# A Mamba-2 layer on one core: the first output block regrouped with fillers and a drain, x's sum forms at other steps, and a dt chain with priority and other banks

## The chip, the core and the metric

The kernel runs on one core of a Trainium2 chip. The metric is the device time of one execution in microseconds (us), the median over runs. The engines in the text are PE (matrix products), DVE (vector operations), ACT (activations), POOL and SP. SP only issues transfers here.

## The reference

One layer of a Mamba-2 mixer over a sequence of L = 512 tokens, all in float32:

```
h = rmsnorm(x)                        # x: 512 x 2048
z, x', B, C, dt = split(h @ w_in)     # 4096, 4096, 8*128, 8*128, 64 columns
x', B, C = silu(conv4(x', B, C))      # causal, 4 taps
dt = softplus(dt + bias)
a = dt * -exp(a_log)                  # decay of each of 64 heads
y = chunked scan: y_diag = (C B^T * exp(cs_l - cs_s)) (x' dt),  y_off = exp(cs) C state
y = rmsnorm((y + D x') * silu(z)) @ w_out
out = rmsnorm(x + y)
```

cs is the running sum of a in a chunk.

## The kernel before, in words

**Numbers.** Each float32 operand is a pair of rounded parts: hi (made by ACT, L88) and lo = value - hi (made by DVE, L89). A product is three matmuls: hi by hi, hi by lo, lo by hi. A weight arrives as a raw piece of 512 KB (buffers ra, rb, rc; three, one and two of them), and `split_piece` splits it. PE can start on a piece when hi is there, and goes on to the third matmul when lo is.

**Order.** PE, SP and POOL follow the order in which the program is written. ACT and DVE are ordered by a scheduler from dependences and priorities; `urgent` raises the priority. The written order is a table of steps: `add(step, function)` puts an event at a step, `run(step)` issues all events of that step between two pieces of PE work. A step is six matmuls, about 0.7 us when PE does not wait.

**The first stage: eight plain tiles** of 128 projection columns each (B, C, x, z, x, z, B, C), two pieces a tile, eight steps a piece. The tiles 2 to 7 begin at step 32, so step 80 begins the second piece of tile 4 and step 120 the second piece of tile 7. Beside them run:

- `x_forms(g, j)`: a quarter of three combinations of x's quadrants (forms 1, 2 and 4), from raw x loaded again: two loads, four ACT scalings, then on DVE L576, L577, L579 and three L574. At steps 49, 56, 63 and 70. `x_form3(j)` makes the fourth form in place over x's right half (L588 to L592), with the conv's buffer xr as scratch, at steps 114, 118, 122 and 126.
- The dt chain: `dt_softplus` at step 58 (L346 to L364), `dt_cumul` at 91 (cs, L372), `dt_sums` at 94 (nwl, win), `dt_spread` at 96 (transposes of cs, copy into sn at L389, store to DRAM as cscr, exponentials, store as escr). These use the one bank of `ps_tr` (tag tr), which xd's transposes (L486) use too.
- Then the first unit's scan: `u_load` brings cscr back, spread over 128 rows, as csb; `u_decay` makes the decay matrix m from it (L469 to L472 on ACT, L474 on DVE). `g_cb` multiplies C by B (cbm, L449).

**The quads** come from step 128 on: pairs of tiles by 2x2 Strassen products (seven instead of eight) over the combined x; T1, T2, T3, R11, R21 and so on name a product. Their weights are sums of pieces (L618).

**The output** (L139): `blocks` is a list of pieces (s, pairs), one accumulation group a tuple, or a pair of tiles by Strassen (`opair`). Of the block's plain groups each of four row tiles t is added into acc (L1065). Between two Strassen pairs the last product of one runs inside the next as filler (`prev`). The combinations of y for the pair are fetched and made by `y_fetch` and `y_forms` (f1, f11 and so on, L860). `load_y(p)` brings y back from DRAM (yscr) and splits it: y2 becomes ybh and ybl.

Of the kernel before, what the change touches and what calls it, by code (L numbers as in the profile page):

```python
# [35 lines left out]
def mamba_layer(ctx: ExitStack, tc: tile.TileContext, d: dict, out: bass.AP):  # L36
# [102 lines left out]
    blocks = [[(0, (0,))] + every(0, 1)[1:] + [(0, (1, 2))] + every(2)[1:], (2, 3), every(3, 12), (4, 5),  # L139
# [234 lines left out]
    def dt_sums():  # L374
        pl = ps_tr.tile([P, NC, H], F32, name="tr")
# [7 lines left out]
    def dt_spread():  # L383
        pct = ps_tr.tile([H, NC, P], F32, name="tr")
# [170 lines left out]
    def x_forms(g, j):  # L555
# [8 lines left out]
        if j == 0:  # L564
# [17 lines left out]

    def x_form3(j):

        kk = slice(2 * j, 2 * j + 2)
        h, lo = xh[:, kk, hi_], xl[:, kk, hi_]
        t = xr[:, 3:L + 3].rearrange("p (k l) -> p k l", k=2)
        V.tensor_tensor(out=t, in0=xh[:, kk, lo_], in1=h, op=ALU.subtract)  # L588
        V.tensor_tensor(out=t, in0=t, in1=xl[:, kk, lo_], op=ALU.add)
        V.tensor_tensor(out=t, in0=t, in1=lo, op=ALU.subtract)  # L590
        S.copy(out=h, in_=t)
        V.tensor_tensor(out=lo, in0=t, in1=h, op=ALU.subtract)  # L592
# [137 lines left out]
    steps = {0: [66, 71, 63, 104, 104, 114], 1: [56, 76, 72, 108, 108, 114], NU - 1: [36, 46, 44, 65, 65, 71]}  # L730
# [298 lines left out]
    for kb, blk in enumerate(blocks[:-1]):  # L1029
# [10 lines left out]
        for s, pairs in blk:  # L1040
            ps = [None] * NC
            for p in pairs:
# [4 lines left out]
                for t in range(NC):  # L1047
# [106 lines left out]
```

## Time and profile before

| | us |
|---|---|
| median of 3 runs (1267.62 to 1270.22) | 1269.15 |
| the profiled execution | 1271.58 |
| its span in the trace | 1269.6 |
| PE busy | 1235.1 (97%) |
| DVE busy | 1079.0 (85%) |
| ACT busy | 829.0 (65%) |
| POOL busy | 77.6 (6%) |

The span is what the trace covers; the 2.0 more of its execution lie around it. A row of the trace gives the start, the duration, the engine, the line, the operation and the tiles (out<-in). In brackets stands the engine's idle time before it and what ended that. PE's clock as granted is 1.00 at full speed; durations of PE are longer where it is lower.

### The profile page before, as it was taken

How to read it: one execution, taken by the hardware profiler on the slowest of the kernel's cores; microseconds unless marked ns; L12 is line 12 of the kernel's file. 1: busy time of each engine (PE TensorE's matmuls, PEld its weight loads, DVE VectorE, ACT ScalarE, POOL GpSimd, SP SyncE). 2: the span in 40 equal slices, each digit the busy share in tenths (PEclk: the TensorE clock that was granted, in tenths of full speed). 3: DMA queues.
4: the chain of work that ended last, by engine and by line, in shares of the span. 5: the costliest groups of instructions: out<-in, count | busy, mean ns of one | idle time of the engine just before them, and what ended most of it. 6: DMA issues, size and time to landing. Idle time of an engine off the chain costs nothing.

```text
span 1269.6 us, 24517 instructions
## 1 busy us (share of the span) xinstructions
PE 1235.1 (97%) x9945; PEld 1178.0 (93%) x9945; DVE 1079.0 (85%) x1443; ACT 829.0 (65%) x1359; POOL 77.6 (6%) x99
## 2 busy tenths in 40 slices
PE   8989899999999999999999999999999899999997
PEld 7989899999999999999999999999888899899986
DVE  5796989998999998899989899988857887887865
ACT  7666677767767767876686777678666445444533
POOL 0000000010000000000001000000000000000000
PEclk9989999999999999999999999999999999999998
DMA  9546656767676667667676766775537576657612
GB/s 357 181 150 180 169 157 174 189 173 193 166 194 182 156 193 189 169 162 197 178 203 151 210 163 176 184 184 153 157 114 253 155 197 202 208 127 229 183 60 100
DMA packets 70193, 225.89 MB, mean 178 GB/s; under 512 B 8384, under 2 KB 12800, under 8 KB 69952
## 3 DMA queue, kind: packets, MB, share of 16 engines
q1 hardware_dynamic: 56688, 176.34, 39.5%
q0 software_dynamic: 12672, 46.14, 23.0%
q8 instruction: 78, 1.28, 0.4%
q10 hardware_dynamic: 720, 1.84, 0.4%
q14 instruction: 35, 0.29, 0.1%
HBM read 211.52 MB, written 12.78 MB: 177 GB/s over the span
## 4 chain that ended last, share of the span: by engine, by line
PE 61%; DVE 19%; ACT 8%; DMA 6%; issue 5%; SPq 0%; DVEq 0%; ACTq 0%
PE S L649 5%; PE S L651 5%; PE S L650 5%; DVE lo L89 4%; PE R L649 4%; PE R L650 3%; PE R L651 3%; PE mm L651 3%; PE mm L649 3%; PE mm L650 3%; PE mm L948 3%; PE mm L950 3%; PE mm L949 3%; PE mm L886 3%; PE mm L887 2%
## 5 line engine op out<-in xcount | busy, mean ns | idle before, releaser
L89 DVE TENSOR_TENSOR lo<-ra,hi 128x1024 fp32r<-128x1024 f32 x150 | 182.8, 1219 | 48.2 <-ACT hi L88 48.0
L88 ACT CAST hi<-ra 128x1024 fp32r<-128x1024 f32 x150 | 156.7, 1046 | 89.9 <-PE mm L887 23.5
L88 ACT CAST hi<-rc 128x1024 fp32r<-128x1024 f32 x94 | 98.9, 1053 | 99.0 <-PE mm L650 37.9
L649 PE MATMUL R<-s,hi 128*128 128x256 f32 x576 | 162.5, 282 | 0.0
L651 PE MATMUL mm<-xh,lo 128*128 128x256 f32 x576 | 159.2, 276 | 0.2 <-DVE lo L89 0.2
L649 PE MATMUL mm<-xh,hi 128*128 128x256 f32 x576 | 159.2, 276 | 0.2 <-ACT mm L705 0.2
L650 PE MATMUL R<-s,hi 128*128 128x256 f32 x576 | 159.2, 276 | 0.0
L651 PE MATMUL R<-s,lo 128*128 128x256 f32 x576 | 159.1, 276 | 0.0
L650 PE MATMUL mm<-xl,hi 128*128 128x256 f32 x576 | 159.1, 276 | 0.0
L89 DVE TENSOR_TENSOR lo<-rc,hi 128x1024 fp32r<-128x1024 f32 x94 | 114.3, 1216 | 3.9 <-ACT hi L88 3.7
L649 PEld LDWEIGHTS mm<-xh,hi 128*128 128x128 f32 x576 | 108.2, 188 | 0.6 <-ACT mm L705 0.6
L651 PEld LDWEIGHTS mm<-xh,lo 128*128 128x128 f32 x576 | 108.1, 188 | 0.4 <-DVE lo L89 0.4
L650 PEld LDWEIGHTS R<-s,hi 128*128 128x128 f32 x576 | 108.3, 188 | 0.0
L649 PEld LDWEIGHTS R<-s,hi 128*128 128x128 f32 x576 | 108.3, 188 | 0.0
L651 PEld LDWEIGHTS R<-s,lo 128*128 128x128 f32 x576 | 108.1, 188 | 0.0
L650 PEld LDWEIGHTS mm<-xl,hi 128*128 128x128 f32 x576 | 108.1, 188 | 0.0
L618 DVE TENSOR_TENSOR ra<-ra,rc 128x1024 f32<-128x1024 f32 x88 | 107.0, 1216 | 0.2
L651 PE MATMUL S<-xh,lo 128*128 128x256 f32 x288 | 79.7, 277 | 2.2 <-DVE lo L89 2.2
L649 PE MATMUL S<-xh,h1h 128*128 128x256 f32 x288 | 80.3, 279 | 1.0 <-ACT mm L705 1.0
L650 PE MATMUL S<-xl,hi 128*128 128x256 f32 x288 | 79.7, 277 | 0.7 <-DVE xl L592 0.7
L650 PE MATMUL S<-xl,h1h 128*128 128x256 f32 x288 | 80.3, 279 | 0.0
L651 PE MATMUL S<-xh,h1l 128*128 128x256 f32 x288 | 80.3, 279 | 0.0
(452 smaller groups left out, 3936.0 us busy)
## 6 DMA issues: line engine op xcount, KB each, us to landing
rc<-in_wi SPq DMA_DIRECT2D x76, 512.0 KB, 5.2
ra<-in_wi SPq DMA_DIRECT2D x42, 512.0 KB, 6.0
rb<-in_wi SPq DMA_DIRECT2D x40, 512.0 KB, 4.6
ra<-in_wi POOLq DMA_DIRECT2D x36, 512.0 KB, 6.2
rb<-in_wi POOLq DMA_DIRECT2D x36, 512.0 KB, 6.2
csb<-cscr SPq DMA_DIRECT2D x32, 512.0 KB, 5.6
ra<-in_wo SPq DMA_DIRECT2D x26, 512.0 KB, 5.2
yscr<-z SPq DMA_DIRECT2D x32, 256.0 KB, 4.4
```

Source lines behind the costliest of these rows:

```text
L88: S.copy(out=hi, in_=raw)
L89: V.tensor_tensor(out=lo, in0=raw, in1=hi, op=ALU.subtract)
L618: V.tensor_tensor(out=raw, in0=raw, in1=qs[n][other], op=ALU.add)
L649: T.matmul(ps, hi[:, k, :], ah, start=first and k == 0, stop=False, skip_group_check=True)
L650: T.matmul(ps, hi[:, k, :], al, start=False, stop=False, skip_group_check=True)
L651: T.matmul(ps, lo[:, k, :], ah, start=False, stop=k == KH - 1, skip_group_check=True)
L886: T.matmul(ps[:, t, :], yh[:, k, tt], hi[:, k, :], start=st, stop=False, skip_group_check=True)
L887: T.matmul(ps[:, t, :], yl[:, k, tt], hi[:, k, :], start=False, stop=False, skip_group_check=True)
L948: T.matmul(ps, yh, hi, start=first and k == 0, stop=False)
L949: T.matmul(ps, yh, lo, start=False, stop=False)
L950: T.matmul(ps, yl, hi, start=False, stop=last and k == 1)
```

## The change

It has three parts.

1. **Output.** The first block's pieces are grouped anew: seven accumulation groups instead of eight, in the order s = 0, 1, 2, 3, 1, 2, 0. The last two tiles of the block's last piece are left out of the block and run inside the first Strassen pair, which so gets a filler (`bridge`) and the product order 11, 1, filler, 2, 4, 12, 3 instead of 1, 11, 4, 2, 12, 3. Its y forms move with the block, as does `load_y(2)`. After the block `T.drain()` stands in place of a spare transpose.
2. **x's forms.** `x_forms` runs at steps 38, 45, 66 and 92 in the order of quarters (1,1), (0,1), (0,0), (1,0). `x_form3` reads raw x, loaded once more by `x_diff` (512 KB at steps 106, 109, 122 and 124, into a buffer ra) and subtracted in place, and needs no scratch. It stands at steps 115, 118, 136 and 140.
3. **dt.** The four parts of the chain run with raised priority. The sums use the bank of `ps_yd`, the spread that of `ps_yo`. `g_cb` for group 0 moves from step 69 to 73, `u_decay` of unit 1 from 140 to 156.

On DVE, where the split of the second piece of tile 4 (lo<-rb) and the copy of cs stand. Before, from the end of dt_softplus on (the split of lo<-rb stands seven rows ahead of this):

```order
L359 SCALAR_TENSOR_TENSOR bt<-bt 128x256
L656 TENSOR_TENSOR z<-S,rbc 128x512
L361 SCALAR_TENSOR_TENSOR dt<-bt,z 128x256
L579 SCALAR_TENSOR_TENSOR rc<-rc,h1l 128x512
L364 SCALAR_TENSOR_TENSOR bt<-dt,dab 128x256
L574 TENSOR_TENSOR s_834<-rc,s_833 128x512
L89 TENSOR_TENSOR lo<-rc,hi 128x1024
L411 TENSOR_TENSOR xr<-mm,rbc 128x512
L574 TENSOR_TENSOR s_836<-rc,s_835 128x512
L401 TENSOR_SCALAR xs<-xr,par 128x512
L89 TENSOR_TENSOR lo<-ra,hi 128x1024
L372 COPY cs<-tr 128x256
```

After; lo<-rb now stands 14 rows ahead of this, and the first row is the split that stood seventh above:

```order
L89 TENSOR_TENSOR lo<-rc,hi 128x1024
L359 SCALAR_TENSOR_TENSOR bt<-bt 128x256
L663 TENSOR_TENSOR z<-S,rbc 128x512
L361 SCALAR_TENSOR_TENSOR dt<-bt,z 128x256
L574 TENSOR_TENSOR s_601<-rc,s_600 128x512
L364 SCALAR_TENSOR_TENSOR bt<-dt,dab 128x256
L411 TENSOR_TENSOR xr<-mm,rbc 128x512
L89 TENSOR_TENSOR lo<-ra,hi 128x1024
L401 TENSOR_SCALAR xs<-xr,par 128x512
L89 TENSOR_TENSOR lo<-ra,hi 128x1024
L404 SCALAR_TENSOR_TENSOR xs<-xr,par,xs 128x512
L372 COPY cs<-tr 128x256
```

The splits moved up past L574 and L579 of x's forms, and one L404 more stands ahead of cs.

On DVE, from the copy of sn to the split of the last plain piece (lo<-rc, step 120). Before:

```order
L389 COPY sn<-tr 64x512
L89 TENSOR_TENSOR lo<-rb,hi 128x1024
L492 TENSOR_TENSOR xw<-xd,win 128x256
L411 TENSOR_TENSOR xr<-mm,rbc 128x512
L401 TENSOR_SCALAR bc<-xr,par 128x512
L404 SCALAR_TENSOR_TENSOR bc<-xr,par,bc 128x512
L474 TENSOR_TENSOR m<-m,cbm 128x1536
L89 TENSOR_TENSOR lo<-rc,hi 128x1024
```

After (the copy of sn stands five rows ahead of these, and a quarter of x's forms lies between):

```order
L492 TENSOR_TENSOR xw<-xd,win 128x256
L89 TENSOR_TENSOR lo<-rb,hi 128x1024
L574 TENSOR_TENSOR s_512<-rc,s_511 128x512
L411 TENSOR_TENSOR xr<-mm,rbc 128x512
L401 TENSOR_SCALAR bc<-xr,par 128x512
L404 SCALAR_TENSOR_TENSOR bc<-xr,par,bc 128x512 x3
L588 TENSOR_TENSOR ra<-ra 128x2x256
L474 TENSOR_TENSOR m<-m,cbm 128x1536
L89 TENSOR_TENSOR lo<-rc,hi 128x1024
```

L588 is now the subtraction of `x_diff`, and it stands ahead of L474; the split stays right behind L474.

On DVE, in the first Strassen output pair. Before (L921 subtracts product R22; L926 subtracts T2, after which T3 may go on in its bank; L971 adds the residual):

```order
L89 TENSOR_TENSOR lo<-rc,hi 128x1024
L89 TENSOR_TENSOR lo<-rb,hi 128x1024
L618 TENSOR_TENSOR ra<-ra,rc 128x1024
L921 TENSOR_TENSOR acc<-acc,mm 128x2x256
L89 TENSOR_TENSOR lo<-ra,hi 128x1024
L926 TENSOR_TENSOR acc<-acc,mm 128x2x256
L618 TENSOR_TENSOR ra<-ra,rc 128x1024
L89 TENSOR_TENSOR lo<-ra,hi 128x1024
L971 SCALAR_TENSOR_TENSOR acc<-xt,rms,acc 128x512
```

After (L1039 is the add of the filler tiles, L938, L933 and L983 are L926, L921 and L971 of before):

```order
L920 TENSOR_TENSOR acc<-acc,mm 128x2x256
L89 TENSOR_TENSOR lo<-rc,hi 128x1024
L1039 TENSOR_TENSOR acc<-mm,acc 128x512 x2
L938 TENSOR_TENSOR acc<-acc,mm 128x2x256
L89 TENSOR_TENSOR lo<-rb,hi 128x1024
L933 TENSOR_TENSOR acc<-acc,mm 128x2x256
L983 SCALAR_TENSOR_TENSOR acc<-xt,rms,acc 128x512
L89 TENSOR_TENSOR lo<-ra,hi 128x1024
```

T2's subtraction (L938) now stands ahead of the splits of lo<-rb and lo<-ra. Before, it stood behind R22's and a lo<-ra.

The diff, cut to its core:

```diff
-    blocks = [[(0, (0,))] + every(0, 1)[1:] + [(0, (1, 2))] + every(2)[1:], (2, 3), every(3, 12), (4, 5),
+    blocks = [[(0, (0,)), (1, (0, 1)), (2, (0, 1)), (3, (0, 1, 2)), (1, (2,)), (2, (2,)), (0, (1, 2))], (2, 3), every(3, 12), (4, 5),
-        late = 4 if i == 0 or i > 2 and type(blocks[i - 1]) is tuple else 0
+        late = 4 if i > 2 and type(blocks[i - 1]) is tuple else 0
     def dt_sums():
-        pl = ps_tr.tile([P, NC, H], F32, name="tr")
+        pl = ps_yd.tile([P, NC, H], F32, name="yd")
     def dt_spread():
-        pct = ps_tr.tile([H, NC, P], F32, name="tr")
+        pct = ps_yo.tile([H, NC, P], F32, name="yo")
+    def x_diff(j, name):
+        raw = load_piece(d["xT"][:, 2 * j:2 * j + 2, :], [P, 2, L], name)
+        V.tensor_tensor(out=raw[:, :, lo_], in0=raw[:, :, lo_], in1=raw[:, :, hi_], op=ALU.subtract)
+        diff[j] = raw[:, :, lo_]
     def x_form3(j):
-        V.tensor_tensor(out=t, in0=xh[:, kk, lo_], in1=h, op=ALU.subtract)
-        V.tensor_tensor(out=t, in0=t, in1=xl[:, kk, lo_], op=ALU.add)
-        V.tensor_tensor(out=t, in0=t, in1=lo, op=ALU.subtract)
-        S.copy(out=h, in_=t)
-        V.tensor_tensor(out=lo, in0=t, in1=h, op=ALU.subtract)
+        t = diff.pop(j)
+        for i in range(2):
+            k = 2 * j + i
+            h, lo = xh[:, k, hi_], xl[:, k, hi_]
+            S.activation(h, t[:, i, :], AF.Identity, scale=lng[:, k:k + 1])
+            V.scalar_tensor_tensor(out=lo, in0=t[:, i, :], scalar=lng[:, k:k + 1], in1=h.bitcast(F32), op0=ALU.mult,
+                                   op1=ALU.subtract)
-    steps = {..., 1: [56, 76, 72, 108, 108, 114], ...}
+    steps = {..., 1: [56, 92, 72, 108, 108, 114], ...}
-        add(49 + 7 * i, x_forms, i // 2, i % 2)
-        add(114 + 4 * i, x_form3, i)
+        add((38, 45, 66, 92)[i], x_forms, *((1, 1), (0, 1), (0, 0), (1, 0))[i])
+        add((106, 109, 122, 124)[i], x_diff, i, "ra")
+        add((115, 118, 136, 140)[i], x_form3, i)
-    add(b0 + 26, dt_softplus)
-    add(b0 + 37, g_cb, 0, 0)
+    add(b0 + 26, hurry, dt_softplus)
+    add(b0 + 41, g_cb, 0, 0)
-    add(b0 + 59, dt_cumul)
-    add(b0 + 62, dt_sums)
-    add(b0 + 64, dt_spread)
+    add(b0 + 59, hurry, dt_cumul)
+    add(b0 + 62, hurry, dt_sums)
+    add(b0 + 64, hurry, dt_spread)
-                q_events(..., base[i] + s * QS, s == 3, 0, 3 if s == 0 and not m else 0, s == 0 and not m)
+                q_events(..., base[i] + s * QS, s == 3, 0, 0, False)
-                add(base[i] - ((50, 32), (54, 32))[m][j], y_fetch, m, j)
-                add(base[i] - ((39, 24), (47, 24))[m][j], y_forms, m, j)
+                add(base[i] - ((54, 36), (54, 32))[m][j], y_fetch, m, j)
+                add(base[i] - ((43, 28), (47, 24))[m][j], y_forms, m, j)
-                    if kb == 2 and n0 + 1 == n_end and t > 1:
+                    if n0 + 1 == n_end and t > 1 and kb < 4:
                         bridge.append(partial(tail, ps[t], opieces[n0], ys[p], t, s))
-                if n0 == 7:
+                if n0 == 6:
                     ph1.close()
                     ...
                     load_y(2)
-                spare = ps_o.tile([P, L], F32, name="mm")
-                T.transpose(spare[:, 0:P], ident, ident)
+                T.drain()
```

`hurry(f)` calls f under raised priority.

More of the change, by code (lines that the diff above doesn't have):

```diff
@@ L563, in x_forms @@
                 S.activation(n[:, i, :], n[:, i, :], AF.Identity, scale=lng[:, k0 + i:k0 + i + 1])
-        if j == 0:
+        if (1, g) not in form:
             for f, s in ((1, 0), (2, 4), (4, 8)):
@@ L581, in x_forms @@
         put(4, t1)
-    def x_form3(j):
-        kk = slice(2 * j, 2 * j + 2)
-        h, lo = xh[:, kk, hi_], xl[:, kk, hi_]
-        t = xr[:, 3:L + 3].rearrange("p (k l) -> p k l", k=2)
-        V.tensor_tensor(out=t, in0=xh[:, kk, lo_], in1=h, op=ALU.subtract)
-        V.tensor_tensor(out=t, in0=t, in1=xl[:, kk, lo_], op=ALU.add)
-        V.tensor_tensor(out=t, in0=t, in1=lo, op=ALU.subtract)
-        S.copy(out=h, in_=t)
-        V.tensor_tensor(out=lo, in0=t, in1=h, op=ALU.subtract)
+    diff = {}
+    def x_diff(j, name):
+        raw = load_piece(d["xT"][:, 2 * j:2 * j + 2, :], [P, 2, L], name)
+        V.tensor_tensor(out=raw[:, :, lo_], in0=raw[:, :, lo_], in1=raw[:, :, hi_], op=ALU.subtract)
+        diff[j] = raw[:, :, lo_]
+    def x_form3(j):
+        t = diff.pop(j)
[5 more added lines that the diff above has]
+                                   op1=ALU.subtract)
     def q_src(n, half, tile_):
@@ L729, in mamba_layer @@
         add(at["x", 4 * g] + 34, g_bt, g)
-    steps = {0: [66, 71, 63, 104, 104, 114], 1: [56, 76, 72, 108, 108, 114], NU - 1: [36, 46, 44, 65, 65, 71]}
+    steps = {0: [66, 71, 63, 104, 104, 114], 1: [56, 92, 72, 108, 108, 114], NU - 1: [36, 46, 44, 65, 65, 71]}
     for u in range(5, NU - 4, UPG):
@@ L783, in mamba_layer, with hurry @@
     st = {}
+    def hurry(f):
+        with urgent():
+            f()
     def norm_a():
@@ L800, in mamba_layer @@
     add(b0 + 44, g_bt, 0)
-    add(b0 + 26, dt_softplus)
-    add(b0 + 37, g_cb, 0, 0)
-    add(b0 + 37, g_cb, 0, 1)
-    add(b0 + 59, dt_cumul)
-    add(b0 + 62, dt_sums)
-    add(b0 + 64, dt_spread)
+    add(b0 + 26, hurry, dt_softplus)
+    add(b0 + 41, g_cb, 0, 0)
+    add(b0 + 41, g_cb, 0, 1)
+    add(b0 + 59, hurry, dt_cumul)
+    add(b0 + 62, hurry, dt_sums)
+    add(b0 + 64, hurry, dt_spread)
     for n in range(2, NPL):
@@ L984, in mamba_layer @@
             for s in range(4):
-                q_events(len(quads) + 4 * m + s, base[i] + s * QS, s == 3, 0, 3 if s == 0 and not m else 0, s == 0 and not m)
+                q_events(len(quads) + 4 * m + s, base[i] + s * QS, s == 3, 0, 0, False)
             for j in range(2):
-                add(base[i] - ((50, 32), (54, 32))[m][j], y_fetch, m, j)
-                add(base[i] - ((39, 24), (47, 24))[m][j], y_forms, m, j)
+                add(base[i] - ((54, 36), (54, 32))[m][j], y_fetch, m, j)
+                add(base[i] - ((43, 28), (47, 24))[m][j], y_forms, m, j)
             m += 1
```

## The prediction

> **What bounds the kernel now.** I read, in this order, the page's first part, the busy times by stage, what PE waited for, the granted clock around those waits, and then single rows where a wait ends. All times below are microseconds of the profiled execution.
>
> ```profile
> PE 1235.1 (97%) x9945; PEld 1178.0 (93%) x9945; DVE 1079.0 (85%) x1443; ACT 829.0 (65%) x1359; POOL 77.6 (6%) x99
> 60.00:90.00 30.00, 26.06 (x197) 25.71 (x196) 27.38 (x49) 22.88 (x34) 0.00 (x0) 0.89 0.51 177
> 90.00:120.00 30.00, 28.35 (x240) 27.77 (x238) 19.42 (x26) 17.11 (x28) 1.00 (x1) 1.00 0.52 156
> 120.00:142.00 22.00, 19.12 (x167) 18.05 (x165) 21.54 (x31) 15.21 (x29) 1.71 (x2) 1.00 0.44 92
> 142.00:171.00 29.00, 26.57 (x221) 25.82 (x221) 25.73 (x36) 19.70 (x34) 2.60 (x3) 0.94 0.76 212
> 200.00:400.00 200.00, 199.54 (x1773) 194.57 (x1772) 182.31 (x236) 146.31 (x249) 15.47 (x18) 1.00 0.69 183
> 987.00:1015.00 28.00, 23.45 (x182) 22.79 (x182) 23.79 (x30) 11.41 (x14) 2.58 (x3) 0.94 0.60 151
> ```
>
> Below the first row each row is a stretch: its length, the busy time (and instructions) of PE, its weight loads, DVE, ACT and POOL, PE's granted clock, the DMA engines' share, GB/s. PE is the bound: 1235.1 of a span of 1269.6, and in the steady stage 199.54 of 200. The change adds no matmul, so it can gain only where PE idles or runs at a reduced clock: the front (60 to 171) and the first Strassen output pair (987 to 1015). There DVE is nearly full as well (27.38 of 30, 21.54 of 22), except from 90 to 120. Time saved at the front stays saved: PE never has slack later to give it back to.
>
> ```profile
> PE tr L486 <- ACT xs L407: 3.1, 8, 1.4
> PE mm L886 <- DVE acc L926: 2.3, 1, 2.3
> PE S L651 <- DVE lo L89: 2.2, 1, 2.2
> PE tr L386 <- DVE xd L489: 1.0, 1, 1.0
> PE S L649 <- ACT mm L705: 1.0, 1, 1.0
> PE S L650 <- DVE xl L592: 0.7, 1, 0.7
> PE tr L486 <- DVE win L379: 0.6, 1, 0.6
> 78.53:85.36 6.83, 6.07 (x28) 0.50 0.93 321
> 139.97:143.38 3.41, 1.69 (x12) 1.00 0.80 171
> 143.38:146.79 3.41, 3.41 (x18) 0.50 1.01 402
> 996.72:1000.13 3.41, 2.06 (x18) 1.00 0.98 316
> 1003.54:1006.95 3.41, 1.15 (x10) 1.00 0.90 323
> 1006.95:1010.37 3.42, 3.42 (x19) 0.50 0.44 107
> ```
>
> The first rows are waits of PE (total, times, longest), the others PE's busy time and granted clock in stretches of 3.41. Half clock comes three times inside the program, in stretches of 3.41 or twice that, the last two right behind one in which PE idled 1.7 or more (3.41 less 1.69; 3.41 less 1.15), the first inside the longest wait; one with 1.35 idle (3.41 less 2.06) brought none. A half-clock stretch costs half its length: 3.41 for the first, 1.71 for each other.
>
> **The front: what goes.** The longest wait is that of step 80, for the second half of a weight piece (lo, tag rb). Its split stood behind work of x's forms and of dt:
>
> ```profile
> 79.29 0.79 PE L211 MATMUL S<-xh,lo 128*128 128x256 f32 x2 [3.94 <-DVE lo L89]
> ...
> 78.02 1.22 DVE L89 TENSOR_TENSOR lo<-rb,hi 128x1024 fp32r<-128x1024 f32 x1
> 90.05 0.42 DVE L372 COPY cs<-tr 128x256 f32<-128x256 f32 x1 [1.27 <-PE tr L370]
> 96.88 0.68 DVE L389 COPY sn<-tr 64x512 f32<-64x512 f32 x1
> ...
> 43.44:97.56 54.12, 50.63 (x85) 0.94 0.43 146
> ```
>
> (The last row is DVE's busy time from the copy of rbc, L308, to the end of sn's copy.) From the copy of rbc to that split DVE's order held 55 instructions and now holds 44: a quarter of x's forms (six of 128x512), two L449 and three L358 stand behind it. By distances from start to start (0.60 for 128x512, as between 1005.32 and 1005.92 in the last rows below; 0.33 for 128x256 and 0.41 for L449 by the same overlap of 0.08) that is 6 x 0.60 + 2 x 0.41 + 3 x 0.33 = 5.4 less, so the split ends near 73.7 instead of 79.15. PE came to the wait at 75.35 (79.29 less 3.94). The wait of 3.94 goes, and with it the half clock (3.41). The 0.6 (L486 behind win) and 1.0 (L386 behind xd) stood at 93 and 96, since the sums and the spread shared the one bank of tag tr with xd's transposes; they get banks of their own: saved too. That is 9.0 by step 112.
>
> **The front: what comes.** What used the stall was the decay chain of the first unit. dt's sums end in the copy of sn; it is stored, loaded spread as csb, twelve ACT instructions and an Exp make m, DVE multiplies m (L474), and right behind it in DVE's order stands the split of piece 15 (lo<-rc), which PE needs at step 120:
>
> ```profile
> 97.59 5.36 DMA cscr<-sn
> 103.02 3.53 DMA csb<-cscr
> 106.65 0.40 ACT L469 ACTIVATE m<-csb,cs 128x128 f32<-128x128 f32 x1 [5.11 <-DMA csb<-cscr]
> 111.25 1.76 DVE L474 TENSOR_TENSOR m<-m,cbm 128x1536 f32<-128x1536 f32 x1 [1.00 <-ACT m L472]
> 112.93 1.22 DVE L89 TENSOR_TENSOR lo<-rc,hi 128x1024 fp32r<-128x1024 f32 x1
> 114.20 0.50 PE L211 MATMUL S<-xh,lo 128*128 128x256 f32 x2
> ```
>
> From sn's end (97.56) to the split's end (114.15) are 16.6, and PE took it at 114.20, with a wait below 0.1. Now PE wants it 9.0 sooner, at 105.2. Is sn 9.0 sooner? From rbc to sn DVE's order held 84 instructions and holds 79: five of 128x512 less, 3.0. DVE idled 54.12 - 50.63 = 3.5 in between, 1.27 of it at cs for PE, which is now ahead. So sn ends between 97.56 - 3.0 = 94.5 (all waits stay) and 91.0 (none stays); I take 91.5, since the largest had PE as its cause and the other quarters' ACT work comes earlier too. The split then ends at 91.5 + 16.6 = 108.1: a **new wait of 2.9** at step 120 (bounds 2.4 to 5.9). By the rows above it is long enough for one half-clock stretch, unless it falls half into each of two: I count 1.7 (bounds 0 and 3.4).
>
> Behind it, in the first quad, x's fourth form was four DVE operations of 128x512 a quarter, and becomes one of 128x512 and two of 128x256: 4 x (4 x 0.60 - 0.60 - 0.66) = 4.6 less on a DVE that was full. The wait for T3's lo (2.2, L651) goes, that for xl (0.7) goes, since the last quarter's load lands about 129.5 for a use at 132 (an estimate by its issue behind the buffer it needs, at 124.5, and a load of 3.5 to 5.4 as above; up to 1 could stay), and 1.0 (L649 behind mm) and 1.4 (the longest of L486 behind xs) were DVE and ACT being late there: gone, with the half clock of 1.71. The four extra loads (512 KB each, 3.53 apiece by csb's, which is as large) are 14 of transfer from step 106 on, where the DMA engines are 0.44 to 0.52 busy and no PE wait above ends with a DMA, so nothing. u_decay of unit 1 sixteen steps later only leaves DVE freer there.
>
> Sum of the front: 3.94 + 3.41 + 0.6 + 1.0 + 2.2 + 0.7 + 1.0 + 1.4 + 1.7 = 16.0 saved, less 2.9 + 1.7: **11.4**.
>
> The Trainium skill, "TensorE: Matmul & The Clock Gate", in "What's actually happening", gives half rate after at least one idle window of about 3.4 us. By that rule the new wait, shorter than a window, would cost no clock, and the forecast would be 1.7 lower; the two stretches above that brought half clock after 1.7 and 2.3 of idle speak against it.
>
> **The output.** The first pair's products were hampered by DVE:
>
> ```profile
> 962.07 1.41 DVE L758 SCALAR_TENSOR_TENSOR ybl<-ra,par,ybh 128x512 fp32r<-128x512 f32 x2
> 964.96 0.39 PE L948 MATMUL mm<-hi,ybh 128*128 128x512 f32 x1
> 986.72 0.28 PE L886 MATMUL mm<-hi,f1h 128*128 128x256 f32 x1
> 1000.90 0.28 PE L886 MATMUL mm<-hi,f12h 128*128 128x256 f32 x1
> 1003.61 0.28 PE L888 MATMUL mm<-lo,f12h 128*128 128x256 f32 x1
> 1004.18 1.23 DVE L89 TENSOR_TENSOR lo<-ra,hi 128x1024 fp32r<-128x1024 f32 x1 [2.04 <-ACT hi L88]
> 1005.32 0.68 DVE L926 TENSOR_TENSOR acc<-acc,mm 128x512 f32<-128x512 f32 x1
> 1005.92 1.22 DVE L618 TENSOR_TENSOR ra<-ra,rc 128x1024 f32<-128x1024 f32 x1
> 1010.58 0.28 PE L886 MATMUL mm<-h1h,f11h 128*128 128x256 f32 x1
> ```
>
> A product without waits took 2.72 (1000.90 to 1003.61 and its last 0.11). Six stand between 986.72 and 1010.58: 6 x 2.72 = 16.3 of 23.9, so 7.5 lost in waits and half clock. L926, which frees a bank, stood behind a split (lo<-ra) that itself waited 2.04. Now four L1065 adds of 128x512 fall away (4 x 0.60 = 2.4 of DVE), the last tiles of the block run as filler between the pair's products (2.72 of PE work that gives DVE time, at no cost since it was done before them), and L926 stands ahead of the splits that wait. I take 7.1 of the 7.5 (bounds 0 and 7.5: 0 if DVE stays behind). The block's order itself moves no matmul; T.drain in place of the spare transpose, some tenth of a microsecond, counts as nothing, since banks are free there. load_y(2) and y2's first use both come one piece earlier (24 matmuls of 128x512, twice the 2.72 of a product's 24 of 128x256: 5.4), while the store it reads does not: ybl was written from 962.07 to 963.5 and used at 964.96, a margin of 1.5 that the store's landing can eat: 0 to 1.5 may be lost; I take 0.
>
> **Sum:** 11.4 + 7.1 = 18.5. The profiled execution (1271.58, 2.4 above the median of 1269.15) would become 1253.1, the median **1250.6**. Differences under 0.2% (2.5) can't be told from none.
>
> **Rivals.**
> - *Little to pay at step 120:* the wait falls half into each of two clock stretches and brings no half clock (1.7 less: 1249), or is itself short (4.6 less: 1246). For it: 1.35 of idle in one stretch brought none, and sn's chain is only 3 late. Against: 1.7 was enough, and store and load (5.36 + 3.53) can't shrink. 0.13.
> - *dt's chain hardly sooner.* sn at 94.5 or later makes the wait 5.9 and two half-clock stretches (3.4): 4.7 more, 1255. For it: DVE is nearly full between 60 and 90. 0.15.
> - *The output pair's gain is lost:* DVE stays behind, or y2 is late: 1256 to 1258. For it: the loads of ra that the split waits for keep their queue. 0.13.
> - *The change doesn't do what it says:* splits moved ahead simply push others late, and only the step 80 wait and its clock go: 1269.15 - 7.4 + 4.6 = 1266. 0.05.
> - *Slower:* one mechanism, the decay chain. Now that hi of piece 15 and its lo both stand behind m, every microsecond by which sn is late falls on PE. With the 18.5 gone once the wait is 2.9 + 18.5 = 21.4, slower begins with sn at 110; a load of csb that queues behind the new loads on SP (3.5 to 5.4 each) would have to wait for all four. 0.05.
>
> My own forecast holds 0.49. From the cases: faster 0.92 (my own, the first three rivals, and half of the fourth, whose 1266 lies at the bound), same 0.03, slower 0.05. The range leaves out the last two rivals and reaches from 1245 (no wait, no half clock, all of 7.5) to 1262 (sn late by 4.7 and the output's gain lost, 1250.6 + 4.7 + 7.1).
>
> **What would show it.** Right: no PE wait on L211 near step 80 and no half clock there; one wait of 2.5 to 6 on L211 at about 105, with L474 as what DVE did just before; DVE's L89 lo<-rc behind L474; no wait on T3 in the first quad; the pair's six products, filler aside, in 16 to 17. Wrong: a wait above 6 at 105, any wait for L598's xl or for x_diff's load, a wait at yb near 955, or PE losing more than a microsecond at the drain.

## Result: 1256.24 us after 1268.43, and where the 12 came from

Beside four runs of the kernel before (1267.62 to 1270.22, median 1268.43) the changed kernel took 1255.53 to 1260.36, median **1256.24**: a ratio of 0.991, 95% interval 0.9889 to 0.9931. The forecast was 1250.6 in 1245 to 1262, a gain of 18.5; the gain is **12.2**. The profiled execution took 1256.68 (span 1255.0).

First the page's busy times and the stretches that answer to those of before (the last row is the first Strassen output pair, which now stands at 974.6 to 994.8):

```profile
PE 1228.0 (98%) x9944; PEld 1171.9 (93%) x9944; DVE 1071.5 (85%) x1435; ACT 828.4 (66%) x1363; POOL 77.7 (6%) x99
```

```profile
60.00:90.00 30.00, 29.70 (x249) 29.17 (x248) 30.00 (x53) 18.32 (x27) 0.54 (x1) 1.00 0.38 125
90.00:120.00 30.00, 22.90 (x185) 22.49 (x184) 19.63 (x29) 19.39 (x35) 0.46 (x1) 0.89 0.54 161
120.00:142.00 22.00, 22.00 (x198) 21.42 (x198) 20.68 (x30) 17.36 (x33) 1.71 (x2) 1.00 0.74 207
142.00:171.00 29.00, 29.00 (x260) 28.42 (x260) 27.37 (x36) 21.84 (x36) 3.45 (x4) 1.00 0.77 215
200.00:400.00 200.00, 199.54 (x1771) 195.17 (x1771) 182.18 (x235) 147.07 (x254) 16.36 (x19) 1.00 0.68 178
974.60:994.80 20.20, 20.09 (x159) 19.23 (x158) 17.19 (x20) 7.75 (x8) 1.73 (x2) 1.00 0.59 161
```

The stall has moved, not only shrunk. From 60 to 90 PE now works 29.70 of 30 at full clock (26.06 at 0.89 before), from 120 to 171 without a gap; but from 90 to 120 it works 22.90 at 0.89, where it had 28.35 at 1.00. DVE is the other side of it: 30.00 of 30 in the stretch from which the wait went. Below, PE's longest waits behind its first 40 us, and then the half clock:

```profile
PE S L211 <- DVE lo L89: 3.9, 1, 3.9
PE S L211 <- ACT hi L88: 3.2, 1, 3.2
PE mm L961 <- DVE lo L89: 1.5, 1, 1.5
```

```profile
105.50:109.74 4.24, 0.74 (x4) 1.00 0.86 328
109.74:116.57 6.83, 3.51 (x16) 0.50 0.18 49
```

Both L211 waits are step 120's, for the hi and then the lo of piece 15: 7.1 where 2.9 was forecast. In the 6.83 at half clock PE was busy for 3.51, so the clock cost 1.75. The third wait is new, behind the second Strassen pair.

Lined up product by product, PE's lead over the kernel before grows like this (the time of before less that of after at the same matmul):

| up to | lead |
|---|---|
| behind step 80 | 6.6 |
| the last product ahead of piece 15 | 8.6 |
| behind step 120 (the first product of the first quad: 119.32 before, 119.82 after) | -0.5 |
| the first product of the third quad (168.21 before, 160.86 after) | 7.35 |
| the end of the steady stage (841.15 before, 833.80 after) | 7.35 |
| the first output block, before its Strassen pair | 9.3 |
| behind the pair's first six products (1010.58 before, 994.75 after) | 15.8 |
| the plain stage behind the whole pair | 13.6 |
| the end of the second pair | 16.4 |
| behind the new L961 wait | 14.5 |
| the span | 14.6 |

At step 120 the changed kernel thus loses its whole lead, and half a microsecond more; all that the front keeps is won behind it, in the first two quads.

The two profiled executions differ by 14.9, the medians by 12.2: before's profiled execution lay 3.15 above its median, after's 0.44. Which part of the 14.9 the median lacks, no trace here shows.

### Why step 120 waits 7.1

The transfers that SP issues, then DVE and ACT around L474, in the changed kernel:

```profile
92.48 0.51 SPq L390 DMA_DIRECT2D cscr<-sn  x1
98.04 0.45 SPq L395 DMA_DIRECT2D escr<-m  x1
98.60 0.52 SPq L453 DMA_DIRECT2D csb<-cscr  x1
101.11 0.59 SPq L82 DMA_DIRECT2D rc<-in_wi  x1
```

```profile
91.78 0.68 DVE L389 COPY sn<-yo 64x512 f32<-64x512 f32 x1
106.39 1.04 ACT L472 ACTIVATE m<-m 128x1024 f32<-128x1024 f32 x1
107.34 1.03 ACT L88 CAST hi<-rc 128x1024 fp32r<-128x1024 f32 x1
109.51 0.69 DVE L588 TENSOR_TENSOR ra<-ra 128x512 f32<-128x512 f32 x1 [6.06 <-DMA ra<-in_xT]
110.12 1.75 DVE L474 TENSOR_TENSOR m<-m,cbm 128x1536 f32<-128x1536 f32 x1
111.79 1.22 DVE L89 TENSOR_TENSOR lo<-rc,hi 128x1024 fp32r<-128x1024 f32 x1
```

- sn ends at 92.46 where 91.5 was taken: 1.0.
- Its store had landed at 96.05, but csb's load was issued at 98.60: on SP it stands behind escr's store, which waited for ACT's exponentials. 2.5. Against that the store took 3.6 and not the 5.36 of before, and the load 4.2 and not 3.53. From sn's end to the first instruction that uses csb it is 10.4 where it was 9.1: 1.3 more.
- m was ready on ACT at 107.43. L474 began at 110.12, because `x_diff`'s subtract (L588) stood ahead of it and sat idle for 6.06 until its raw x had landed. 2.7.
- The split ends at 113.0 where 108.1 was forecast: 4.9 late, which is 1.0 + 1.3 + 2.7 but for 0.1. PE works 0.74 of that time, between its two waits.
- A link outside this chain is late as well: the raw load of piece 15 itself (the last SP row) stands behind csb's on SP and landed at 106.64, when PE had been at the piece since 105.2. With ACT's 1.03 for hi, 2.4 of the wait would have been there whatever m did.

### The profile page after: what moved, and what is told of

Read it like the earlier page. It is cut to its first block, busy times and chain, and to the rows that moved or that the text cites. A ratio compares the mean times of both kernels' runs of the same rounds, so it can differ in the third digit from the quotient of the medians.

```text
span 1255.0 us, 24524 instructions
## 1 busy us (share of the span) xinstructions
PE 1228.0 (98%) x9944; PEld 1171.9 (93%) x9944; DVE 1071.5 (85%) x1435; ACT 828.4 (66%) x1363; POOL 77.7 (6%) x99
## 4 chain that ended last, share of the span: by engine, by line
PE 62%; DVE 17%; ACT 8%; DMA 7%; issue 5%; SPq 0%; DVEq 0%; ACTq 0%
PE S L658 5%; PE S L657 5%; PE S L656 5%; PE R L656 4%; PE R L657 4%; PE R L658 4%; DVE lo L89 4%; PE mm L658 3%; PE mm L657 3%; PE mm L656 3%; PE mm L960 3%; PE mm L962 3%; PE mm L961 3%; PE mm L898 3%; PE mm L899 3%
## 5 line engine op out<-in xcount | busy, mean ns | idle before, releaser
L658 PEld LDWEIGHTS mm<-xh,lo 128*128 128x128 f32 x576 | 108.1, 188 | 0.3 <-DVE lo L89 0.3
L656 PEld LDWEIGHTS mm<-xh,hi 128*128 128x128 f32 x576 | 108.1, 188 | 0.0
L657 PEld LDWEIGHTS mm<-xl,hi 128*128 128x128 f32 x576 | 108.1, 188 | 0.0
L658 PEld LDWEIGHTS R<-s,lo 128*128 128x128 f32 x576 | 108.1, 188 | 0.0
L658 PE MATMUL S<-s,lo 128*128 128x256 f32 x288 | 79.5, 276 | 0.0
L656 PE MATMUL S<-s,hi 128*128 128x256 f32 x288 | 79.5, 276 | 0.0
```

What stands on the lines that cost most here:

```text
L656: T.matmul(ps, hi[:, k, :], ah, start=first and k == 0, stop=False, skip_group_check=True)
L657: T.matmul(ps, hi[:, k, :], al, start=False, stop=False, skip_group_check=True)
L658: T.matmul(ps, lo[:, k, :], ah, start=False, stop=k == KH - 1, skip_group_check=True)
```

## Experiments

Two theories stood at the start. One: the wait is 7.1 because of csb's place on SP and the subtract's on DVE, and each put right gives back 2.5 or more. The rival: the front is so full that a wait taken away there comes back as the next late thing. Single parts undone then say what each part of the change brings. The times of a kernel are compared with before on the same chip.

The same front ran in four profiled executions (the changed kernel twice, and two variants that differ only in the output stage). In these the first product of the third quad starts at 159.29, 160.78, 160.86 and 162.05. This start is the marker below: its place in the other experiments is read against these 159.3 to 162.1. (The first product of the second quad, nearer to the "end of the first quad" of the expectations, starts at 137.4 to 139.8 in the four.) Step 120 is not alike in them: PE waits 6.08, 6.62, 7.10 and 5.91 there, and the half clock costs 1.8, 2.9, 1.75 and 3.4.

### The two causes

**e1: the subtract later.**

```diff
-        add((106, 109, 122, 124)[i], x_diff, i, "ra")
-        add((115, 118, 136, 140)[i], x_form3, i)
+        add((112, 114, 122, 124)[i], x_diff, i, "ra")
+        add((121, 124, 136, 140)[i], x_form3, i)
```

> The changed kernel with x_diff of the first two quarters at steps 112 and 114 (not 106, 109) and their x_form3 at 121 and 124, so that DVE's order has L474 and the split of piece 15 ahead of the subtraction that waits for raw x. Theory Q (two in-order queues made the wait at step 120 7.1 instead of 2.9): m was ready at 107.43, so L474 and the split end at about 110.3 instead of 113.0; the wait at step 120 falls from 7.1 to about 4.4 and the median by about 2.7, to 1253.5. Rival C (the chain from sn to m is simply that long, the subtraction only stood next to it): the wait stays at 7 and the median at 1256 within 1.

Measured: 1262.17, ratio 0.9946 (0.9928 to 0.9964). DVE's L474 and a later wait of PE:

```profile
107.10 1.76 DVE L474 TENSOR_TENSOR m<-m,cbm 128x1536 f32<-128x1536 f32 x1 [3.79 <-ACT m L472]
...
138.00 0.38 PE L656 MATMUL S<-xh,hi 128*128 128x256 f32 x1 [1.79 <-ACT xh L597]
```

L474 now waits for m itself, and step 120 waits 2.98 + 0.77 = 3.75 in place of 7.1. So the subtract did cost 3.3 there, or 2.2 against the shortest wait of the unchanged front (5.91). But x's last quarter comes late for PE: 1.79 for xh and 0.26 for xl, and a half clock of 3.41 behind them. At step 120 the half clock itself costs 3.0, since PE now works through all but 0.78 of the 6.83. The marker stands at 163.18, 1.1 past the latest of the unchanged front. What was saved at 105 was given back by 142, and more. The wait did what the first theory said; the time met neither expectation.

**e2: csb's load ahead of escr's store**, on SP, for the first unit:

```diff
+        csb0.append(sp.tile([P, 2, L], F32, name="csb"))
+        nc.sync.dma_start(csb0[0], cscr[0:2, :].partition_broadcast(P))
```

These stand between the two stores of `dt_spread`; `u_load` then takes this tile for unit 0 (the line numbers are 5 higher behind it).

> The changed kernel with unit 0's load of csb written right behind the store of cscr, ahead of the store of escr in SP's order (DVE's order then has L474 and the split ahead of the subtraction too). Theory Q: cscr landed at 96.05 but csb's load was issued at 98.60, behind escr's store, which waited for ACT. It now goes out near 96.1, m is ready 2.5 sooner (104.9), and then the landing of piece 15 itself (106.64) sets hi (107.6) and lo (108.8): the wait at step 120 falls from 7.1 to about 3.2, the median by about 4, to 1252. Rival C: store and load of the chain are bound by their own latency; m comes less than 0.5 sooner and the median falls by less than 1.

Measured: 1264.12, ratio 0.9964 (0.9949 to 0.998). The issue on SP, and two of PE's waits:

```profile
96.98 0.34 SPq L394 DMA_DIRECT2D csb<-cscr  x1
98.90 0.46 SPq L399 DMA_DIRECT2D escr<-m  x1
102.98 0.59 SPq L82 DMA_DIRECT2D rc<-in_wi  x1
```

```profile
PE S L661 <- ACT xh L602: 2.4, 1, 2.4
PE S L661 <- ACT sn L707: 1.8, 1, 1.8
```

csb leaves 1.6 earlier and step 120 waits 2.10 + 0.32. This is not the price of csb's place alone. On DVE the subtract now stands behind L474 and the split too (110.17), so both causes are gone at once; and though csb landed at 100.39, m was ready only 0.9 sooner (106.49), because its buffer held the exponentials until escr's store had landed at 101.81. What is left of the wait is the raw load of piece 15, which landed at 107.62. Then 1.8 (T3, whose bank ACT must first copy into sn), 2.4 for xh and 1.6 for xl follow, and the marker is at 166.50, 5.6 later than in the changed kernel. Waits of 4.7 went and 5.8 came, and half clock of 3.41 at 109 and 6.83 at 140, most of it with PE at work. Here too the time met neither expectation.

**e3: piece 15 first.** Its split is raised in priority, and the first unit's load and decay matrix move to steps 105 and 106 (line numbers 4 higher):

```diff
-            pieces[n] = split_piece(raw, WSH, wp)
+            if n == 15:
+                with urgent():
+                    pieces[n] = split_piece(raw, WSH, wp)
+            else:
+                pieces[n] = split_piece(raw, WSH, wp)
-    steps = {0: [66, 71, 63, 104, 104, 114], ...}
+    steps = {0: [73, 74, 63, 104, 104, 114], ...}
```

> The changed kernel with u_load and u_decay of unit 0 at steps 105 and 106 (98 and 103 before), so that piece 15's load stands ahead of csb's on SP, and piece 15's split with raised priority, so that it no longer stands behind m on ACT and DVE. Theory Q: the load goes out at 98.6 instead of 101.1 and lands near 104, hi is ready at 105.1 and lo at 106.2: a wait of about 1 instead of 7.1 at step 120 and no half clock there: 6 and 1.7 less, median about 1248.5. Rival S (the split only changes places: the decay of unit 0 or the sums of the first quad's weights come late instead): the wait at step 120 goes, but 3 or more of it come back in the first quad, median 1252 to 1254.

Measured: 1263.39, ratio 0.9958 (0.9943 to 0.9973). Step 120 has no wait. A later product waits instead:

```profile
131.49 0.58 PE L662 MATMUL mm<-xh,lo 128*128 128x256 f32 x1 [3.38 <-DVE lo L89]
```

With it come 1.0 for xl, 1.0 (L490) and 0.7 for xh, and 6.83 at half clock from 130.7. Marker 163.84. The rival is right in kind: all of the 7.1 can be taken away and the kernel is slower for it, at 1263 and not the 1252 to 1254 that it expected.

### The next late thing put right as well

In the changed kernel itself the last quarter's raw x waited for the third quarter's buffer ra, and landed at 135.77:

```profile
131.79 0.33 SPq L82 DMA_DIRECT2D ra<-in_xT  x1
```

The prediction had put that at 129.5; that it cost no wait is owed to PE, which step 120 had held 4 us longer. Two kernels, e6 on top of e2 and e7 on top of e3, give this load the buffer rc and its form an earlier place:

```diff
-        add((106, 109, 122, 124)[i], x_diff, i, "ra")
-        add((115, 118, 136, 140)[i], x_form3, i)
+        add((106, 109, 122, 124)[i], x_diff, i, ('ra', 'ra', 'ra', 'rc')[i])
+        add((115, 118, 128, 132)[i], x_form3, i)
```

> The kernel of e2 (csb's load ahead of escr's store) with the last quarter's raw x in a buffer rc instead of ra, and x_form3 of the last two quarters at 128 and 132 (not 136, 140). In e1 and e2 the wait at step 120 fell from 7.1 to 3.75 and 2.4, but the first product that uses the last quarter then waited 2.1 and 4.0, since its load waited for the third quarter's buffer. Theory L (that load is what is late next): it goes out near 126 instead of 131.8, the waits for xh and xl in the first quad go (below 0.5 in sum), and PE is 4 to 5 further by the end of the first quad than in the changed kernel. Rival D (DVE and ACT are full there, and the saving would be given back in any case): as much as 2 or more is waited for another split or copy in the first quad, and PE is within 2 of the changed kernel.

Measured: 1259.98, ratio 0.9917 (0.9892 to 0.9943), the marker at 162.07. The waits for xh and xl are gone, as expected of them. Step 120 waits 3.71 + 0.52, again for the raw load of piece 15 (landed at 108.87, m ready at 107.64), and 2.2 (T3 behind the copy into sn) and 1.9 (L491 behind xs) stand in the new places. Its chain began late: a load of x's second quarter landed at 55.14 (53.41 in the repeat below), and DVE's idle time at 55 grew from 2.32 to 3.94. With DVE's row full until 90, nothing behind it makes that up. By its interval this time can't be told from that of the changed kernel.

> The kernel of e3 (piece 15 loaded and split ahead of the decay chain) with the same other buffer and steps for the last quarter. In e3 the 7.1 at step 120 were gone and 3.4 came back at a split in the first quad that stood behind xl's last parts, and 1.7 for xh and xl. Theory L: the split of lo<-rc (row 141 of DVE's order) still stands behind the third quarter, whose load is unchanged, so 2 to 3 of wait remain there, but xh and xl bring none: PE is 3 to 4 further than in e3. Rival D: the waits only move, PE is within 1 of e3.

Measured: 1261.77, ratio 0.994 (0.9919 to 0.9961), marker 161.76:

```profile
PE mm L662 <- DVE lo L89: 4.2, 2, 4.0
```

PE still waits for the quad's split (L662), now 4.0, so the wait of e3 was not x's doing. The first product of the second quad comes at 138.51, 3.4 sooner than in e3 as expected, and the marker 2.1 sooner.

**e5: the same kernel again**, beside these two:

> The changed kernel, unchanged, beside the others on one chip. Matmuls of 128x256 follow each other at 113.3 ns in some stretches and at 117.8 in others; between the profiled executions of the changed kernel and of e1 (whose programs are alike from unit 1 on) the steady stage differs by 4.3 by that alone. Theory X (the pace is drawn anew in each execution): the steady stage of this execution has another number of slow matmuls than the 73 of the first profile, and the median over ten runs lies above 1256, near 1259. Rival K (the pace is fixed by the program): again 70 to 80 slow ones, the first output pair slow and the second fast, median 1256 within 1.

Measured: 1257.57, ratio 0.9892 (0.9868 to 0.9915). Step 120 waits 2.83 + 3.25, so the 7.1 is itself one draw of several. Over both sets the eight runs of the changed kernel have a median of 1256.8.

**e9: the quarters of x's forms in another order**, so that the second one's buffers are free sooner:

```diff
-        add((38, 45, 66, 92)[i], x_forms, *((1, 1), (0, 1), (0, 0), (1, 0))[i])
+        add((38, 45, 66, 92)[i], x_forms, *((1, 1), (0, 0), (0, 1), (1, 0))[i])
```

> The changed kernel with the second and third quarter of x_forms exchanged: (1,1), (0,0), (0,1), (1,0), so that the quarter of step 45 loads into csb and m and no longer waits for h1h and h1l of the first. Theory B (the front is bound by DVE's row, and DVE idled 2.3 to 3.9 at L576 near 55 for the second load of that quarter): the idle goes, sn and m come about 2.4 sooner, the wait at step 120 is 2 to 3 shorter than 6 to 7, PE is 2 to 4 further by the end of the first quad, median about 1254. Rival D (the saving is given back at the next transfer): PE is within 1 of the changed kernel there, the median stays at 1256 to 1258.

Measured: 1258.03, ratio 0.9906 (0.989 to 0.9922): level with the changed kernel. The marker is at 158.94, DVE's idle at 57 is 0.80, sn ends at 91.20 (92.46 and, in the repeat, 91.82 in the changed kernel), and there is no half clock between the program's start and its end. Yet PE's waits are, the first row at 64 and 70 and the second at step 120:

```profile
PE mm L211 <- DVE lo L89: 2.1, 2, 1.7
PE S L211 <- DVE lo L89: 2.1, 1, 2.1
PE S L656 <- ACT sn L702: 1.6, 1, 1.6
```

and a subtract sits idle even longer, ahead of the rest of DVE's row:

```profile
104.19 0.69 DVE L588 TENSOR_TENSOR ra<-ra 128x512 f32<-128x512 f32 x1 [8.92 <-DMA ra<-in_xT]
```

Seven waits of 0.4 to 2.1 take the place of two long ones. The time is the rival's.

### Each part undone alone

**e4: the output as before**, the rest as changed (the diff of part 1 reversed, with the spare transpose):

```diff
-    blocks = [[(0, (0,)), (1, (0, 1)), (2, (0, 1)), (3, (0, 1, 2)), (1, (2,)), (2, (2,)), (0, (1, 2))], (2, 3), ...
+    blocks = [[(0, (0,))] + every(0, 1)[1:] + [(0, (1, 2))] + every(2)[1:], (2, 3), ...
-                T.drain()
+                spare = ps_o.tile([P, L], F32, name="mm")
+                T.transpose(spare[:, 0:P], ident, ident)
```

> The changed kernel with the output part undone: blocks, late, the steps of y_fetch and y_forms, the products' order, load_y(2) at the seventh piece and the spare transpose as before; x's forms and dt as changed. Theory O (the output part brought the 5.9 that the first pair gained by the traces): the median rises by 5 to 7, to about 1262; the first pair's six products take about 24 again. Rival F (the first pair would have run better anyway, since its waits hang on when the loads come): they take 17 to 19, and the median rises by less than 2.

Measured: 1261.39, ratio 0.9946 (0.9924 to 0.9967). The six products take 21.3 (979.26 to 1000.57), with

```profile
989.97 0.39 PE L900 MATMUL mm<-lo,f2h 128*128 128x256 f32 x1 [1.34 <-DVE lo L89]
```

and a half clock of 3.41, where before took 23.9. Medians put the output part at 4.6, less than the 6.5 of the pair alone in the lead above: the pair of before was disturbed more (23.9) than with the changed front (21.3).

**e10: x_forms at the steps of before:**

```diff
-        add((38, 45, 66, 92)[i], x_forms, *((1, 1), (0, 1), (0, 0), (1, 0))[i])
+        add(49 + 7 * i, x_forms, i // 2, i % 2)
```

> The changed kernel with x_forms at steps 49, 56, 63, 70 in the order of before, all else as changed. Theory M (the moved quarters took the wait at step 80 away): the wait of 3.9 at step 80 and the half clock of 3.4 come back, sn ends 3 to 5 later but PE is later too, so that the wait at step 120 is 3 to 7: median 5 to 7 above the changed kernel, near 1263. Rival P (the priority of the dt chain did it): no wait over 1 at step 80, median within 2 of the changed kernel.

Measured: 1263.29, ratio 0.9955 (0.9938 to 0.9971). The step 80 wait is back, longer than the 3.94 of before, with 6.83 at half clock; step 120 waits 0.21:

```profile
80.93 0.58 PE L211 MATMUL S<-xh,lo 128*128 128x256 f32 x1 [6.46 <-DVE lo L89]
```

So the steps and order of x's forms alone move the wait between step 80 and step 120. Marker 165.03.

**e11: x's fourth form as before, without `x_diff`:**

```diff
-        add((106, 109, 122, 124)[i], x_diff, i, "ra")
-        add((115, 118, 136, 140)[i], x_form3, i)
+        add(114 + 4 * i, x_form3, i)
```

> The changed kernel with x_form3 of before (in place from xh and xl, steps 114 to 126, no x_diff). Theory Q: no subtraction that waits for raw x stands ahead of L474, so the wait at step 120 falls to about 4.4; but DVE has 4.6 more to do in the first quad, and waits for T3's split, xl and xs come back (up to 2.2 + 0.7 + 1.0 + 1.4 and a half clock of 1.7): PE at the end of the first quad 2 to 5 behind the changed kernel, median near 1260. Rival N (the rewritten form brings nothing): PE is level or ahead there, median 1255 to 1257.

Measured: 1265.7, ratio 0.9964 (0.995 to 0.9978), marker 167.30. Without the subtract step 120 waits 2.48 + 0.77 = 3.25, close to the 2.9 forecast. The quad pays:

```profile
156.46 0.48 PE L486 MATMUL tr<-ident,xs 128*128 128x128 f32 x1 [5.32 <-ACT xs L407]
```

and 3.41 at half clock, in the second quad: at its first product PE was still level (137.57). The new fourth form is thus the dearest part to leave out, and the one whose subtract lengthens step 120.

**e12: dt without priority, its sums in the bank of before:**

```diff
-        pl = ps_yd.tile([P, NC, H], F32, name="yd")
+        pl = ps_tr.tile([P, NC, H], F32, name="tr")
-        pct = ps_yo.tile([H, NC, P], F32, name="yo")
+        pct = ps_tr.tile([H, NC, P], F32, name="tr")
-        with urgent():
-            f()
+        f()
```

> The changed kernel without the raised priority of the dt chain and with its sums and spread in ps_tr again. By the prediction's terms the waits of 0.6 and 1.0 (L486 behind win, L386 behind xd) come back, 1.6 in all, and sn comes 1 to 3 later, which lengthens the wait at step 120 by as much less 1.6: median 2 to 4 above the changed kernel, 1259 to 1261. Rival P (priority carries the front): the copy of cs and sn fall back by 5 or more and the wait at step 120 is over 10. Rival N: less than 1 in all.

Measured: 1260.42, ratio 0.993 (0.9912 to 0.9948), marker 165.53.

```profile
PE tr L370 <- DVE bt L364: 4.2, 1, 4.2
PE S L211 <- DVE lo L89: 3.2, 1, 3.2
PE tr L486 <- DVE win L379: 0.5, 1, 0.5
PE tr L386 <- DVE xd L489: 0.5, 1, 0.5
```

The size is near the expected one, the place is not. PE waits 4.2 at L370, where it sums up dt, and 0.5 twice for the shared bank; step 120 got no longer (3.2), and PE comes to it later by what it lost at L370. Its interval and those of the changed kernel overlap, so it is the marker, not the time, that sets it apart.

Undone singly, the parts cost 4.6, 6.5, 8.9 and 3.6 by medians against 1256.8: 23.6 (1.4 to 1.7 of each is the pace told of below, and each interval above is about 2 wide to either side), where all together bring some 12. In the front alone the marker says the same: 4.3, 6.5 and 4.8 against the mean of the four unchanged fronts (160.75), 15.6, where all three bring 7.5. By these rows each part needs the others: what it saves is lost again at another late thing if that isn't moved too.

### Two speeds of the same matmul

**e8:** a drain ahead of each of the 56 products of the Strassen output pairs, to see what a drain costs and whether a product's pace changes with PE's stops:

```diff
+        T.drain()
```

> The changed kernel with a drain of PE ahead of each of the 56 products of the output pairs, to see what sets the pace of 113.3 or 117.8. Theory R (a pace is taken up at each restart of PE and kept until the next): after 56 drains both paces appear among the products, changing from product to product. Rival B (the pace belongs to a stage of the execution, not to a restart): all 28 products of a pair keep one pace. A drain costs about 0.2, so 11 in all, time near 1268.

Measured: one run of 1276.87, some 20 above the changed kernel: 0.36 a drain, if all of it is the drains. From the start of one product to that of the next the trace has 0.34 to 0.50 (median 0.38) more than 24 matmuls at their pace. The change's own drain, behind the filler in each of the two pairs, thus counts for less than the runs can tell. Of 55 products whose pace could be read, 18 ran their matmuls at 117.8 ns from start to start and 37 at 113.3, and each kept to one pace but for its first matmuls. What that means for the comparison stands in the last section.

No kernel tried beats the changed one; e9 is level with it, and the intervals alone don't set e6, e7 and e12 apart from it.

## Why the prediction was right in direction and too high by 6

**The front: what goes (9.0): right but for 0.4.** All four terms went (0.3 of waits is left from 60 to 90), and the lead at the last product ahead of piece 15 is 8.6. The half clock was put at 3.41, but by the prediction's own row PE worked only 6.07 of those 6.83; the rest is counted in the wait already, so it cost 3.0. (That PE came at 105.2, the very number, is a coincidence: it came there for hi, where 105.2 had been worked out for lo, which it uses 0.56 later.) The split of step 80 ended in time:

```profile
72.20 1.21 DVE L89 TENSOR_TENSOR lo<-rb,hi 128x1024 fp32r<-128x1024 f32 x1
```

73.41 against the forecast 73.7, for a use at 75.35.

**"sn ends between 94.5 and 91.0; I take 91.5": 92.46.** Within its bounds, 1.0 off. The idle time that was to go is partly still there:

```profile
55.51 0.69 DVE L576 TENSOR_TENSOR rc<-h1l,h1h 128x512 f32<-128x512 f32 x1 [2.43 <-ACT h1l L563]
```

**"A new wait of 2.9 (bounds 2.4 to 5.9)": 7.1, wrong, and the failed term.** The 16.6 from sn to the split was carried over from before as if its links had no company; it took 20.55. Two links had company. The load of csb got an issue behind a store that waited for ACT, and the subtract stood ahead of L474. e1 shows the second (3.75 without it), and e11, which has no subtract, leaves 3.25. The first is shown less well: its net 1.3 stands in the trace, but e2 removed both at once. That "store and load (5.36 + 3.53) can't shrink" was wrong as well, the store took 3.6. And one thing was not followed at all: piece 15's own raw load, too late by itself for 2.4 of the wait. e3 moved that load and the split ahead of the chain, and no wait was left. The step that failed reads "the four extra loads ... so nothing". The transfers were costed against the DMA engines' share; that DVE would stand still behind one, 6.06 long, with PE's split two rows below, was not. The order's excerpt showed L588 ahead of L474.

**The half clock, 1.7: 1.75, right by luck.** One stretch of 3.41 with PE at work was forecast. Two came, and PE sat idle through 3.32 of the first; the other three executions of this front paid 1.8, 2.9 and 3.4. The Trainium skill, "TensorE: Matmul & The Clock Gate", in "What's actually happening", has half rate come after at least one idle window of about 3.4. Here it came at 109.74, behind a stretch in which PE had worked 0.74 between its two waits; in e11 it came behind a wait of 2.48, in e1 behind one of 1.79. By that rule none of these would have brought half rate.

**Behind step 120 (2.2 + 0.7 + 1.0 + 1.4 + 1.7 = 7.0): 7.85, right,** read from the lead (-0.5 to 7.35): these waits and the half clock are gone, and the rest lies at the stops, each of which cost PE 0.1 to 0.25 beyond its wait. (T3's wait, xl's and 1.0 stood in the first quad and at the start of the second, the 1.4 at 159 in the second.) But "the last quarter's load lands about 129.5" was wrong by 6: it waits for the buffer of the third quarter, whose last reader ends at 131.77:

```profile
130.89 0.88 DVE L598 SCALAR_TENSOR_TENSOR xl<-ra,lng,xh 128x256 fp32r<-128x256 f32 x2
135.80 0.69 DVE L588 TENSOR_TENSOR ra<-ra 128x512 f32<-128x512 f32 x1 [0.79 <-DMA ra<-in_xT]
```

So the term for xl was right by luck: where e1 and e2 shortened step 120, the wait for x was there. Had step 120 been 2.9 as forecast, some of it would probably have come, and the sum of 11.4 would not have been reached.

**The output (7.1 of 7.5): 6.5.** The pair now runs from 974.68 (its first f11) to 994.75 (the next), 20.07 with the filler in it; before, the six products took 23.86 and the filler's work 2.72 ahead of them, 26.58:

```profile
994.75 0.28 PE L898 MATMUL mm<-h1h,f11h 128*128 128x256 f32 x1
997.58 0.28 PE L898 MATMUL mm<-hi,f1h 128*128 128x256 f32 x1
1000.41 0.28 PE L898 MATMUL mm<-hi,f22h 128*128 128x256 f32 x1
```

No wait is left in it, so the mechanism held. The missing 0.6 is a slip in the sum: the row that was to give 2.72 a product gives 2.82 (1000.90 to 1003.61 is 2.71, and 0.11 more), as a product takes here (2.83, 997.58 less 994.75). So 6.9 could be won, not 7.5. y2 came in time, and the drain cost 0.27: the filler's last matmul and the next product start 0.50 apart, where the matmuls follow each other at 0.23.

**What the sum did not have:** 2.0 in the block ahead of the pair (a wait of 0.64 gone and 0.75 of pace among them), 2.2 lost in the rest of the pair and 2.8 won up to the end of the second, nearly all by pace, and 1.9 lost around a new wait of 1.46:

```profile
1176.85 0.50 PE L961 MATMUL mm<-lo,yah 128*128 128x512 f32 x1 [1.46 <-DVE lo L89]
```

**From the profile to the median.** The sum comes to 14.6 of span instead of 18.5: 4.05 less in the front, 0.6 less in the pair, and small terms of both signs. The rest of the miss is not a stage: the 2.4 by which before's profiled execution lay above its median was taken off after's as well, which lay only 0.44 above its own.

Nearest of the rivals was "dt's chain hardly sooner" (a wait of 5.9, 1255), right in size though not in its cause.

## What to carry to other kernels

When work is moved off a full in-order row, follow every instruction that stays ahead of the critical one and ask what *it* waits for: a subtract that costs 0.69 cost 2.2 to 3.3 because it waited for a load two rows ahead of PE's split. Do the same for the queue that issues transfers, the critical piece's own load first, and for the buffer that a load needs before it can start. And where PE and DVE are both full, price a part by undoing it too: parts that share one stretch have no prices of their own, and curing the longest wait alone (e1, e2, e3) made the front end 1.1 to 4.5 us later than the latest of the four that left it.

## What the runs showed of the hardware

**One matmul, two paces.** A 128x256 product with its weight load starts every 113.3 or every 117.8 ns at full granted clock, and the trace shows which by the duration, 276 or 281 ns. One product of the pairs (f2h in before, f12h in after and its repeat; minimum, median and maximum of a group, then its first and last start), in the first and the second Strassen pair of before, then of after, and in the first of the repeat:

```profile
L886 PE MATMUL mm<-hi,f2h x24: 276/276/276, 1018.8 to 1059.2; 128*128 128x256 f32 x24
...
L886 PE MATMUL mm<-hi,f2h x16: 281/281/281, 1160.3 to 1182.5; 128*128 128x256 f32 x16
```

```profile
L898 PE MATMUL mm<-hi,f12h x8: 281/281/281, 989.1 to 991.6; 128*128 128x256 f32 x8
...
L898 PE MATMUL mm<-hi,f12h x16: 276/276/276, 1150.5 to 1171.9; 128*128 128x256 f32 x16
```

```profile
L898 PE MATMUL mm<-hi,f12h x8: 276/276/276, 987.3 to 989.7; 128*128 128x256 f32 x8
```

Two executions of one kernel differ in it, and in e8 it changed from product to product, where PE had stopped. In the steady stage of about 5140 such matmuls before had 72 slow ones, the changed kernel 73 and 70, the ten other kernels without e8's drains 388 to 894, at 4.5 ns each: 1.4 to 3.7 us of what they lost to the changed kernel is this. Whether the code draws the pace or chance does, and what sets it, stays open.

**Half clock** came always in multiples of 3.41, after single waits of 1.79 (e1, 0.26 more close behind), 2.10 (e2), 2.48 (e11) and longer; 2.06 in e9 brought none. So neither the wait's length nor a whole idle stretch decides it alone. Where the idle time lies does: within an execution all half clocks start on one grid of 3.413 (in before 78.53, 143.38 and 1006.96 are 19 and 253 stretches apart). Cut all fourteen traces into the stretches of their own grid, from 25 to 1235. Each of the 18 at full clock in which PE was idle for 2.05 or more was followed by half clock, none of those with 1.49 or less was, and of the eight from 1.56 to 1.86 two were (1.56 in e4, 1.72 in before). The 2.06 of e9 lies across two stretches, 0.84 in the one and 1.22 in the other. Its two stretches, then that of e4:

```profile
104.28:107.70 3.42, 2.58 (x23) 1.00 0.06 24
107.70:111.11 3.41, 2.19 (x19) 1.00 0.00 0
987.28:990.69 3.41, 1.85 (x14) 1.00 0.72 252
```

So the prediction's 1.7 is near the limit but not the limit: 1.75 in before, in the stretch from 136.56, brought none. What decides between 1.56 and 1.86 stays open; PE's busy time is modelled at its ends.
